# A hybrid decoder block on one core: first half's expert lists paced more slowly, prefix products held behind the sums, first column group read in pairs, selection matrices moved to VectorE

## The chip, the cores and the metric

The kernel runs on one core of a Trainium2 chip. The metric is device time in microseconds (us). TensorE does the matrix products (PE in the rows, PEld its weight loads), VectorE (DVE), ScalarE (ACT) and GpSimd (POOL) the elementwise work, and SyncE (SP) issues most loads. GpSimd also issues the gathers from the expert table.

## The reference

One decoder layer in float32 on 1024 tokens of width 1024. The query width of the expert part is 8 heads x 256.

```
mod = silu(c) @ w_ada + b_ada                      # 6 x 1024: shift, scale, gate, twice
h = modulate(rms_norm(x), shift1, scale1);  proj = h @ w_in
# GLA branch, gMLP branch, sigmoid gates of proj -> merged
x = x + gate1 * (merged @ w_out)
h2 = modulate(rms_norm(x), shift2, scale2)
q = h2 @ w_q                                       # 8 heads, two halves of 128
s1, s2 = q[..., 0, :] @ keys1.T, q[..., 1, :] @ keys2.T     # 128 keys each
idx, g = 16 best of the pairs (top16(s1) + top16(s2)), softmax
u, v = expert_down[idx], expert_up[idx]            # 16384 experts of width 1024
x = x + gate2 * sum(g * gelu(u . h2) * v);  return rms_norm(x)
```

## The kernel before

**Halves.** The tokens are worked in two halves of 512, each four blocks of 128. A half first runs the projection `w_in` in 14 column groups of 512, then the output projection (two parts, `w_out_part`), the second norm (`h2_part`), and the query projection `w_q(q)` in four column groups (`q=0` in two halves of 256 tokens, the others on 512). A column group has eight k-steps (`stream`, `group`): a 128x512 weight tile `wt` is loaded, ScalarE rounds it to `wh` (L1037), GpSimd or VectorE makes the rest `wl` (L1039), and TensorE does twelve products in `mm3` (L173 to L175), so that the float32 product is made of three faster ones. After each k-step `step()` lets four queues go on, each by a credit that the table `rate` gives per step.

**Experts.** Behind a half's query projection `s_part` makes the scores (L1395) and `tops` their best; `rank(b)` puts `routing(b)` of a block into the routing queue, and, at the last block of a group of blocks, `rare(gi)`. The groups are (0,1,2,3), (4,5) and (6,7). Each head's best expert of a token is a direct entry: it is gathered row by row, its dot product is one DVE instruction (L452), and its sum uses the diagonal matrix `Wd`. All other pairs are packed into lists of up to 128 pairs, ten per block; a prefix sum over the 128 partitions gives each pair its place, and the part of it across partitions is the product with `ltri` (L263 in `routing`'s packing and in that of the rare lists, L336 in `rare`). What many tokens of a group share goes through `rare` and its own lists; their result comes back as `yr`, one row in each block's stream.

A list entry takes a selection matrix `E` (L593: a distance `ea` made by ScalarE is compared with a bound), products of `h2` and of the list with `E` (L494, L495, L464, L465), the dot products on VectorE (L496), the gather (L442), a second matrix `e` (L485, named `e2` in the code) that puts its rows back to their tokens, and the sum.

**Two ways of summing.** `peer_stream` goes through one list of entries, `todo`, strictly in its order: the six rare lists of the first group, the lists of blocks 0 to 3 (each closed by its `yr` entry), then for each later group the direct entries, four rare lists, and the lists of its two blocks. The first half's entries run inside the second half's projection, by the credits `RP` (in the projection), `RP2` (output projection and on) and `RP3` (last three query groups). They use small buffers, two entries ahead, and `split_add` (L523 to L526), which splits the gathered values into two parts for faster products. Behind the projection `peer_pools("1", …, True)` opens larger buffers ("own"): seven entries ahead and `add_rows` (L515), float32 products. In own `E`, `e` and `Wr` were made on GpSimd; in the small pool `E` is made on VectorE.

**Start.** `ada_cols(k)` makes the shift and scale of the first norm for 128 columns: it loads 128-column pieces of `w_ada` in runs of 512 bytes, multiplies and adds them on VectorE (L913), and sums over partitions by TensorE. It is called once for each k of the first column group, which cannot pass k before.

The scheduler sets the order on each engine ahead of time; `tc.issue_after(ins)` keeps an instruction behind `ins` on its engine.

Of the kernel before, what the change touches and what calls it, by code (L numbers as in the profile page):

```python
# [54 lines left out]
RP = .42  # L55
RP2 = .42
DA = 8
FP = 15
EP = (True,)
# [9 lines left out]
RP3 = .5  # L69
AS = 1  # L70
# [15 lines left out]
def block_kernel(ctx: ExitStack, tc: tile.TileContext, x, xT, cT, w_ada, b_ada, b_adaT, n1T, w_inp, w_alr,  # L86
# [80 lines left out]

    def split_psum(hi, lo, ps):
        nc.scalar.activation(hi, ps, AF.Identity)  # L169
        nc.vector.tensor_tensor(lo, ps, hi.bitcast(F32), op=OP.subtract)  # L170

    def mm3(ps, lh, ll, rh, rl, first, last):
        nc.tensor.matmul(ps, lh, rh, start=first, stop=False)  # L173
        nc.tensor.matmul(ps, lh, rl, start=False, stop=False)  # L174
        return nc.tensor.matmul(ps, ll, rh, start=False, stop=last).ins  # L175
# [78 lines left out]
    def pack_list(tsel, n, col, rps, tag):  # L254
# [8 lines left out]
        nc.tensor.matmul(pst, ltri, cnt[:, col:col + 1], start=True, stop=True)  # L263
# [62 lines left out]
    def rare(gi, rps):  # L326
# [7 lines left out]
        nc.vector.tensor_copy(cnt[:, col:col + 1], inc[:, n - 1:n])  # L334
        pst = rps.tile([P, 1], F32, name="aux", tag="aux")
        nc.tensor.matmul(pst, ltri, cnt[:, col:col + 1], start=True, stop=True)  # L336
# [122 lines left out]
    def entry_list(pl, ul, Ej, blk):  # L459
# [25 lines left out]
        nc.gpsimd.tensor_scalar(e2, iota[:, int(lane0(b)):int(lane0(b)) + P], ts_[:, 3 * n:3 * n + 1], None, op0=OP.is_equal)  # L485
# [25 lines left out]
    def add_rows(wv, acc, first, last):  # L511
        W, v = wv
        for n in range(2):
            sl = slice(n * 512, (n + 1) * 512)
            nc.tensor.matmul(acc[:, sl], W, v[:, sl], start=first, stop=last)  # L515

    def split_add(ent, acc, first, last):
        pl, _, _, r, uv, _, e2 = ent
        for n in range(2):
# [6 lines left out]
            nc.tensor.matmul(acc[:, sl], e2, vl, start=False, stop=last)  # L526

    def rare_rows(pl, ul, b):
# [4 lines left out]
        nc.gpsimd.tensor_scalar(W, iota[:, :P], rcol[gi][:, bi:bi + 1], None, op0=OP.is_equal)  # L533
# [52 lines left out]
    def peer_E(pl, pb, j):  # L586
# [6 lines left out]
        (nc.gpsimd if pl["own"] in EP else nc.vector).tensor_scalar(E[:, :n], ea[:, :n], hw[:, 1:2], None, op0=OP.is_le)  # L593
# [52 lines left out]
    def peer_stream(bs):  # L646
# [190 lines left out]
    with ExitStack() as pa:  # L837
# [58 lines left out]
        def ada_cols(k):  # L896
            accs = []
            for hf_ in range(2):
                wa = t4("wada").rearrange("p (a c f) -> p a c f", a=4, c=2)
                src = w_ada[hf_ * 512:(hf_ + 1) * 512, :].rearrange("(a p) n -> p a n", p=P)  # L900
                for c in range(2):
                    nc.sync.dma_start(wa[:, :, c], src[:, :, c * D + k * P:c * D + (k + 1) * P])
                acc = gl.tile([P, 2, P], F32, name="adc", bufs=4)
                for a in range(4):
                    w_, s_ = wa[:, a], sc[:, 4 * hf_ + a:4 * hf_ + a + 1]
                    if a < AS:
                        nc.scalar.activation(acc if a == 0 else w_, w_, AF.Identity, scale=s_)
                        if a:
                            nc.gpsimd.tensor_tensor(acc, acc, w_, op=OP.add)
                    elif a == 0:  # L910
                        nc.vector.tensor_scalar(acc, w_, s_, None, op0=OP.mult)
                    else:
                        nc.vector.scalar_tensor_tensor(acc, w_, s_, acc, op0=OP.mult, op1=OP.add)  # L913
                accs.append(acc)
            ps = auxt([P, 2])
            for c in range(2):
                for i, acc in enumerate(accs):
                    nc.tensor.matmul(ps[:, c:c + 1], acc[:, c], ones[:, 0:1], start=i == 0, stop=i == 1)
            nc.vector.tensor_tensor(mod[:, k:16:KD], ps, badat[:, k:16:KD], op=OP.add)
            nc.vector.scalar_tensor_tensor(scol[:, k:k + 1], mod[:, KD + k:KD + k + 1], 1.0, n1t[:, k:k + 1],  # L920
# [80 lines left out]
        def h_first(k):  # L1001
            if k + 1 < KD:
# [491 lines left out]
```

## Time and profile before

| | |
|---|---|
| runs of the kernel (us) | 1672.44, 1666.29, 1671.41; median 1671.41 |
| the profiled execution (us) | 1661.6, of which the span is 1659.9 |
| mean granted clock of TensorE | 0.936 of full speed |
| busy | PE 1438.1 (87%), DVE 1070.9, POOL 887.5, ACT 778.0 |

The profiled execution is 9.8 us under the median of the runs. The span runs from the first to the last instruction; the granted clock is a share of TensorE's full speed.

### The profile page before, as it was taken

How to read it: one execution, taken by the hardware profiler on the slowest of the kernel's cores; microseconds unless marked ns; L12 is line 12 of the kernel's file. 1: busy time of each engine (PE TensorE's matmuls, PEld its weight loads, DVE VectorE, ACT ScalarE, POOL GpSimd, SP SyncE). 2: the span in 40 equal slices, each digit the busy share in tenths (PEclk: the TensorE clock that was granted, in tenths of full speed). 3: DMA queues.
4: the chain of work that ended last, by engine and by line, in shares of the span. 5: the costliest groups of instructions: out<-in, count | busy, mean ns of one | idle time of the engine just before them, and what ended most of it. 6: DMA issues, size and time to landing. Idle time of an engine off the chain costs nothing. (4 is left out here: it accounts for less than half of the span.)

```text
span 1659.9 us, 20529 instructions
## 1 busy us (share of the span) xinstructions
PE 1438.1 (87%) x6113; PEld 1078.2 (65%) x6113; DVE 1070.9 (65%) x2862; ACT 778.0 (47%) x1716; POOL 887.5 (53%) x761
## 2 busy tenths in 40 slices
PE   4999889999998998788889999989789954798894
PEld 2768757888768886567667777767578832353452
DVE  6773654111456469977987778788885476576653
ACT  4453323332446355735446665555455344444442
POOL 4232237543375338756666877556575425655750
PEclk7999989999999999999999999989899975899998
DMA  9643533223377338746756788768756364897992
GB/s 272 235 175 98 173 121 106 93 91 133 101 241 256 119 115 295 251 153 230 260 188 204 282 319 295 281 213 300 275 213 230 114 232 155 346 415 274 410 412 89
DMA packets 132635, 363.83 MB, mean 219 GB/s; under 512 B 17577, under 2 KB 36265, under 8 KB 116386
## 3 DMA queue, kind: packets, MB, share of 16 engines
q0 software_dynamic: 30816, 178.14, 28.5%
q1 hardware_dynamic: 78464, 132.15, 24.2%
q10 hardware_dynamic: 23234, 52.14, 8.8%
q8 instruction: 49, 0.80, 0.2%
q14 instruction: 72, 0.59, 0.1%
HBM read 336.44 MB, written 25.94 MB: 218 GB/s over the span
## 5 line engine op out<-in xcount | busy, mean ns | idle before, releaser
L1039 POOL TENSOR_TENSOR wl<-wt,wh 128x512 fp32r<-128x512 f32 x257 | 364.3, 1424 | 386.5 <-ACT wh L1037 328.1
L174 PE MATMUL mm<-wl,hTh 128*128 128x512 f32 x896 | 366.3, 409 | 10.3 <-DVE wl L1039 5.6
L1037 ACT ACTIVATE wh<-wt 128x512 fp32r<-128x512 f32 x368 | 228.4, 627 | 308.1 <-PE mm L175 184.8
L175 PE MATMUL mm<-wh,hTl 128*128 128x512 f32 x896 | 357.4, 404 | 3.0 <-DVE hTl L996 3.0
L173 PE MATMUL mm<-wh,hTh 128*128 128x512 f32 x896 | 339.5, 413 | 20.2 <-DVE sg L1240 6.4
L173 PEld LDWEIGHTS mm<-wh,hTh 128*128 128x128 f32 x896 | 172.8, 194 | 71.8 <-DVE sg L1240 7.7
L174 PEld LDWEIGHTS mm<-wl,hTh 128*128 128x128 f32 x896 | 173.2, 193 | 59.2 <-POOL wl L1039 9.2
L1039 DVE TENSOR_TENSOR wl<-wt,wh 128x512 fp32r<-128x512 f32 x111 | 100.0, 903 | 158.6 <-ACT wh L1037 146.4
L175 PEld LDWEIGHTS mm<-wh,hTl 128*128 128x128 f32 x896 | 172.6, 193 | 43.3 <-DVE hTl L996 3.1
L173 PE MATMUL mm<-hTh,wh 128*128 128x512 f32 (+1 forms) x448 | 167.2, 375 | 18.7 <-ACT hTh L169 6.4
L175 PE MATMUL mm<-hTh,wl 128*128 128x512 f32 (+1 forms) x448 | 158.2, 371 | 9.7 <-POOL wl L1039 7.2
L174 PE MATMUL mm<-hTl,wh 128*128 128x512 f32 (+1 forms) x448 | 163.9, 366 | 0.0
L442 POOL DMA_INDIRECT uv<-in_tab_dram,ix x94 | 102.7, 1093 | 71.6 <-PE acc L515 24.4
L496 DVE SCALAR_TENSOR_TENSOR uv<-uv,hps 128x512 f32<-128x512 f32 x148 | 97.8, 683 | 54.6 <-PE hps L495 33.3
L524 DVE SCALAR_TENSOR_TENSOR vl<-uv,r,vh 128x512 fp32r<-128x512 f32 x92 | 91.8, 1026 | 34.7 <-ACT vh L523 29.5
L173 PEld LDWEIGHTS mm<-hTh,wh 128*128 128x128 f32 x448 | 86.4, 194 | 35.4 <-ACT hTh L169 7.1
L515 PE MATMUL acc<-uv,W 128*128 128x512 f32 x192 | 98.9, 641 | 4.4 <-ACT W L508 2.9
L175 PEld LDWEIGHTS mm<-hTh,wl 128*128 128x128 f32 x448 | 85.6, 193 | 24.3 <-POOL wl L1039 8.2
L174 PEld LDWEIGHTS mm<-hTl,wh 128*128 128x128 f32 x448 | 86.5, 193 | 13.5 <-DVE hTl L170 0.2
L494 PE MATMUL hps<-hh,E 128*128 128x512 f32 x148 | 77.8, 529 | 17.7 <-DVE uv L496 12.3
L515 PE MATMUL acc<-uv,Wd 128*128 128x512 f32 x128 | 61.3, 628 | 9.1 <-ACT Wd L456 7.2
L186 DVE MAX8 tv<-so 128x8 f32<-128x128 f32 x128 | 28.5, 277 | 62.1 <-ACT so L1397 62.1
(955 smaller groups left out, 2727.9 us busy)
## 6 DMA issues: line engine op xcount, KB each, us to landing
wt<-in_w_inp_dram SPq DMA_DIRECT2D x224, 256.0 KB
wt<-in_w_qp_dram SPq DMA_DIRECT2D x80, 256.0 KB
wada<-in_w_ada_dram SPq DMA_DIRECT2D x32, 512.0 KB
wt<-in_w_outp_dram SPq DMA_DIRECT2D x64, 256.0 KB
wada<-in_w_ada_dram SPq DMA_DIRECT2D x32, 256.0 KB
s_d<-so ACTq DMA_DIRECT2D x32, 256.0 KB
xr<-in_x_dram ACTq DMA_DIRECT2D x8, 512.0 KB
x_d<-x ACTq DMA_DIRECT2D x8, 512.0 KB
```

What stands on the lines that cost most here:

```text
L173: nc.tensor.matmul(ps, lh, rh, start=first, stop=False)
L174: nc.tensor.matmul(ps, lh, rl, start=False, stop=False)
L175: return nc.tensor.matmul(ps, ll, rh, start=False, stop=last).ins
L186: nc.vector.max(v, st)
L442: nc.gpsimd.indirect_dma_start(out=uv[:], out_offset=None, in_=tab, in_offset=bass.IndirectOffsetOnAxis(ap=ix, axis=0))
L494: nc.tensor.matmul(hps, Ej, hh[:, sl], start=True, stop=False)
L496: nc.vector.scalar_tensor_tensor(uv[:, sl], uv[:, sl], 1.0, hps, op0=OP.mult, op1=OP.mult, accum_out=r[:, 2 + n:3 + n])
L515: nc.tensor.matmul(acc[:, sl], W, v[:, sl], start=first, stop=last)
L524: nc.vector.scalar_tensor_tensor(vl, v, r[:, 5:6], vh.bitcast(F32), op0=OP.mult, op1=OP.subtract)
L1037: nc.scalar.activation(wh, wt, AF.Identity)
L1039: eng.tensor_tensor(wl, wt, wh.bitcast(F32), op=OP.subtract)
```

## The change

Six pieces are changed.

1. The credits of the first half's lists go from .42, .42 and .5 to .33, .33 and .3 per step.
2. In own, `E`, `e` and `Wr` are made on VectorE.
3. The products with `ltri` are issued behind the last product that the program wrote before them (a matmul of `mm3`, or a sum), and `rare` yields once ahead of its own.
4. Entries are prepared as far ahead as the buffers of their own block allow, so the first half's last entries stay two ahead behind the projection's end too.
5. `ada_cols` makes 256 columns at a time: 1 KB runs, 128x512 instructions, four calls in place of eight.
6. In the second half, the last query group runs in two halves of 256 tokens, and each half's blocks are ranked at once.

```diff
-RP = .42
-RP2 = .42
+RP = .33
+RP2 = .33
-RP3 = .5
-AS = 1
+RP3 = .3
...
+        last_pe[:] = [nc.tensor.matmul(ps, ll, rh, start=False, stop=last).ins]
+        return last_pe[0]
...
         pst = rps.tile([P, 1], F32, name="aux", tag="aux")
-        nc.tensor.matmul(pst, ltri, cnt[:, col:col + 1], start=True, stop=True)
+        with tc.issue_after(last_pe[0]):
+            nc.tensor.matmul(pst, ltri, cnt[:, col:col + 1], start=True, stop=True)
...
-        nc.gpsimd.tensor_scalar(e2, iota[:, int(lane0(b)):int(lane0(b)) + P], ts_[:, 3 * n:3 * n + 1], None, op0=OP.is_equal)
+        (nc.vector if own else nc.gpsimd).tensor_scalar(e2, iota[:, int(lane0(b)):int(lane0(b)) + P], ts_[:, 3 * n:3 * n + 1], None, op0=OP.is_equal)
...
-        (nc.gpsimd if pl["own"] in EP else nc.vector).tensor_scalar(E[:, :n], ea[:, :n], hw[:, 1:2], None, op0=OP.is_le)
+        nc.vector.tensor_scalar(E[:, :n], ea[:, :n], hw[:, 1:2], None, op0=OP.is_le)
...
         def fill(nxt, k):
-            while nxt < len(todo) and nxt <= k + use[-1]["ahead"]:
+            while nxt < len(todo):
                 b, j = todo[nxt]
+                pl = preps[b][0] if b in preps else use[-1]
+                if nxt > k + pl["ahead"]:
+                    break
...
+        def ada_cols(kp):
             accs = []
+            w2 = 2 * P
             for hf_ in range(2):
+                acc = gl.tile([P, 2, w2], F32, name="adc", bufs=3)
                 for a in range(4):
+                    q = 4 * hf_ + a
+                    if a % 2 == 0:
+                        wa = t4("wada").rearrange("p (a c f) -> p a c f", a=2, c=2)
...
+                    else:
+                        nc.vector.scalar_tensor_tensor(acc, wa[:, a % 2], sc[:, q:q + 1], acc, op0=OP.mult, op1=OP.add)
...
+                for p in (0, 1) if hf and q == 3 else (None,):
+                    w_q(q, p)
+                    if q == 3:
+                        for i in range(BH) if p is None else (2 * p, 2 * p + 1):
+                            rank(blks[i])
...
-            for b in blks:
-                rank(b)
```

TensorE at the end of the second half's projection, before: the last product of the query projection, all scores (`aux<-keyst,qt`), then the first prefix products and direct sums (`Wd`), and at the bottom the first list entry of the later groups.

```order
L175 MATMUL mm<-hTh,wl 128x512
L1395 MATMUL aux<-keyst,qt 128x128 x16
L263 MATMUL aux<-cnt,ltri 128x1
L515 MATMUL acc<-uv,Wd 128x512 x10
L263 MATMUL aux<-cnt,ltri 128x1
L336 MATMUL aux<-cnt,ltri 128x1
L515 MATMUL acc<-uv,Wd 128x512 x4
L349 MATMUL tpq<-tq,qE 128x20
```

The same place in the changed kernel: behind the last product come the scores of two blocks, and then products of the first half's entries (`e_11585` is the matrix of one of them).

```order
L175 MATMUL mm<-hTh,wl 128x256
L1403 MATMUL aux<-keyst,qt 128x128 x8
L529 MATMUL acc<-vh,e_11585 128x512
L530 MATMUL acc<-vl,e_11585 128x512
L529 MATMUL acc<-vh,e_11585 128x512
L468 MATMUL tps<-thl,E 128x170
```

Some sixty rows on, after seven such entries in all, stands the end of the first half's stream (`yr`), and only behind it `rare`'s product (L340, which was L336), the direct sums and the first list of the later groups.

```order
L530 MATMUL acc<-vl,e_12286 128x512
L519 MATMUL acc<-yr,Wr 128x512 x2
L340 MATMUL aux<-cnt,ltri 128x1
L353 MATMUL tpq<-tq,qE 128x20
L519 MATMUL acc<-uv,Wd 128x512 x14
L265 MATMUL aux<-cnt,ltri 128x1
L519 MATMUL acc<-uv,Wd 128x512 x2
L498 MATMUL hps<-hh,E 128x512
```

So seven list entries and one `yr` entry that stood among the projection's products now stand behind the last of them, and the chain of `rare` behind those. The scores of blocks 4 and 5 still stand behind all products of both token halves.

GpSimd in the lists of the last groups, before: gathers (`uv<-in_tab_dram`) alternate with `E` and `e`.

```order
L442 DMA uv<-in_tab_dram,dix_148 128x2048
L166 TENSOR_TENSOR fs<-fs,mhalf 128x1
L593 TENSOR_SCALAR E<-ea,hw 128x256 x3
L442 DMA uv<-in_tab_dram,dix_148 128x2048
L593 TENSOR_SCALAR E<-ea,hw 128x256
L442 DMA uv<-in_tab_dram,dix_148 128x2048
L485 TENSOR_SCALAR e_13719<-iota,ts__13709 128x128
L485 TENSOR_SCALAR e_13741<-iota,ts__13731 128x128
L442 DMA uv<-in_tab_dram,ix 128x2048
```

The same stretch of GpSimd after:

```order
L446 DMA uv<-in_tab_dram,ix 128x2048
L446 DMA uv<-in_tab_dram,dix_148 128x2048 x3
L164 TENSOR_TENSOR fs<-fs,mhalf 128x1
L446 DMA uv<-in_tab_dram,dix_148 128x2048 x5
L277 TENSOR_TENSOR tlq<-qtsel,thq 128x32
L164 TENSOR_TENSOR fs<-fs,mhalf 128x1
L446 DMA uv<-in_tab_dram,ix 128x2048
L446 DMA uv<-in_tab_dram,dix_149 128x2048 x2
```

Gathers and three small instructions are left on GpSimd there. The matrices stand on VectorE now, between the dot products of the lists (L500, which was L496).

```order
L500 SCALAR_TENSOR_TENSOR uv,r<-uv,hps 128x512
L489 TENSOR_SCALAR e_14488<-iota,ts__14478 128x128
L474 SCALAR_TENSOR_TENSOR jk,r<-ts__14538,slot_65 128x56
L500 SCALAR_TENSOR_TENSOR uv,r<-uv,hps 128x512
L486 SCALAR_TENSOR_TENSOR jk,r<-ts__14538,slot_65 128x56
L500 SCALAR_TENSOR_TENSOR uv,r<-uv,hps 128x512
L489 TENSOR_SCALAR e_14509<-iota,ts__14499 128x128
```

Here two `e` of 128x128 stand where VectorE had dot products and `jk` alone.

## Rows read from the trace of the kernel before

**Rows 1.** The page's busy us, share of the span and instructions of each engine.

```profile
PE 1438.1 (87%) x6113; PEld 1078.2 (65%) x6113; DVE 1070.9 (65%) x2862; ACT 778.0 (47%) x1716; POOL 887.5 (53%) x761
```

**Rows 2.** Windows by stage: busy us (instructions) of each engine, clock, DMA share, GB/s.

```profile
30.00:46.00 16.00, 11.06 (x28) 8.29 (x29) 15.97 (x23) 7.42 (x13) 11.09 (x8) 0.50 0.79 224
46.00:75.00 29.00, 29.00 (x148) 22.49 (x146) 19.27 (x39) 16.20 (x27) 6.85 (x10) 0.99 0.64 225
250.00:417.00 167.00, 163.32 (x726) 131.69 (x725) 36.26 (x66) 55.82 (x86) 87.56 (x65) 0.99 0.32 106
417.00:510.00 93.00, 81.78 (x357) 63.66 (x356) 50.58 (x64) 43.08 (x75) 45.54 (x35) 0.95 0.56 190
...
870.00:1060.00 190.00, 179.53 (x801) 143.09 (x800) 145.49 (x306) 115.14 (x276) 136.43 (x116) 0.98 0.80 292
1060.00:1250.00 190.00, 161.54 (x764) 128.13 (x763) 164.52 (x295) 106.30 (x227) 120.70 (x91) 0.93 0.68 239
1250.00:1337.00 87.00, 86.49 (x432) 72.04 (x430) 38.72 (x187) 36.12 (x68) 37.16 (x29) 1.00 0.44 153
1337.00:1392.00 55.00, 19.77 (x42) 8.17 (x42) 45.68 (x294) 27.39 (x68) 18.51 (x30) 0.68 0.51 191
1392.00:1440.00 48.00, 32.67 (x87) 20.08 (x88) 30.21 (x149) 22.37 (x78) 35.45 (x37) 0.69 0.78 297
1440.00:1500.00 60.00, 57.78 (x178) 31.20 (x177) 40.23 (x186) 26.85 (x85) 33.38 (x39) 1.00 1.01 413
1500.00:1560.00 60.00, 47.70 (x129) 23.72 (x127) 37.19 (x125) 27.44 (x95) 40.60 (x43) 0.89 0.83 315
1560.00:1608.00 48.00, 45.03 (x134) 22.83 (x132) 27.77 (x97) 22.13 (x74) 27.88 (x30) 1.00 1.01 421
1608.00:1650.00 42.00, 29.45 (x84) 15.01 (x82) 20.62 (x48) 12.21 (x34) 5.96 (x8) 0.93 0.48 183
```

**Rows 3.** Groups of the first 46 us by line: busy us, mean ns, idle before.

```profile
L913 DVE SCALAR_TENSOR_TENSOR adc<-wada,sc,adc 128x256 f32<-128x256 f32 x29 | 19.8, 731 | 1.7 <-ACT adc L907 1.7
```

**Rows 4.** TensorE's timeline at the projection's end: start, us, line, idle before and releaser.

```profile
1334.90 2.05 PE L1395 MATMUL aux<-keyst,qt 128*128 128x128 f32 x16 [0.46 <-ACT so L1397]
1353.31 0.56 PE L263 MATMUL aux<-cnt,ltri 128*128 128x1 f32 x2 [16.35 <-DVE cnt L260]
1353.73 10.81 PE L515 MATMUL acc<-uv,Wd 128*128 128x512 f32 x20
...
1365.52 0.36 PE L336 MATMUL aux<-cnt,ltri 128*128 128x1 f32 x2
...
1388.51 0.59 PE L263 MATMUL aux<-cnt,ltri 128*128 128x1 f32 x2 [11.46 <-DVE cnt L260]
1391.96 0.80 PE L494 MATMUL hps<-hh,E 128*128 128x512 f32 x1 [2.87 <-POOL E L593]
```

**Rows 5.** Groups of VectorE, 870 to 1250 us.

```profile
L524 DVE SCALAR_TENSOR_TENSOR vl<-uv,r,vh 128x512 fp32r<-128x512 f32 x84 | 84.8, 1036 | 29.7 <-ACT vh L523 24.4 <-PE acc L526 2.9 <-PE acc L525 1.4
...
L593 DVE TENSOR_SCALAR E<-ea,hw 128x128 fp32r<-128x128 f32 x40 | 23.0, 576 | 3.2 <-PE hps L495 2.1 <-ACT ea L592 1.1
```

**Rows 6.** Groups of TensorE, 870 to 1250 us: products of the halved column group.

```profile
L173 PE MATMUL mm<-hTh,wh 128*128 128x256 f32 x64 | 18.8, 297 | 7.4 <-DVE hTl L170 5.3 <-ACT hTh L169 2.2
```

**Rows 7.** Groups behind 1392 us, GpSimd, VectorE and TensorE.

```profile
L593 POOL TENSOR_SCALAR E<-ea,hw 128x256 fp32r<-128x256 f32 x23 | 25.8, 1122 | 4.0 <-ACT ea L592 3.6 <-PE hps L495 0.2
L485 POOL TENSOR_SCALAR e<-iota,ts__12915 128x128 f32<-128x128 f32 x1 | 2.5, 2527 | 0.0
L496 DVE SCALAR_TENSOR_TENSOR uv<-uv,hps 128x512 f32<-128x512 f32 x96 | 63.3, 684 | 34.7 <-PE hps L495 21.2 <-DMA uv<-in_tab_dram,ix 13.1 <-issue 0.2
```

**Rows 8.** Waits, 1392 to 1440 us, then 1500 to 1560 us: total, times, longest.

```profile
ACT ea L592 <- POOL E L593: 7.1, 5, 2.2
...
ACT ea L592 <- POOL E L593: 11.8, 7, 2.3
```

**Rows 9.** One line of VectorE (comparison with a constant, 128x128): min, median, max ns.

```profile
L345 DVE TENSOR_SCALAR qlt<-iota,qse x3: 266/280/288, 768.9 to 1456.9; 128x128 f32<-128x128 f32 x3
```

More of the change, by code (lines that the diff above doesn't have):

```diff
@@ L514, in add_rows @@
             sl = slice(n * 512, (n + 1) * 512)
-            nc.tensor.matmul(acc[:, sl], W, v[:, sl], start=first, stop=last)
+            last_pe[:] = [nc.tensor.matmul(acc[:, sl], W, v[:, sl], start=first, stop=last).ins]
     def split_add(ent, acc, first, last):
@@ L532, in rare_rows @@
         W = pl["pq"].tile([P, P], F32, name="Wr", tag="e2", bufs=pl["ahead"] + 2)
-        nc.gpsimd.tensor_scalar(W, iota[:, :P], rcol[gi][:, bi:bi + 1], None, op0=OP.is_equal)
+        (nc.vector if pl["own"] else nc.gpsimd).tensor_scalar(W, iota[:, :P], rcol[gi][:, bi:bi + 1], None, op0=OP.is_equal)
         return W, y
@@ L894, in ada_acc @@
                 yield acc
-        def ada_cols(k):
+        def ada_cols(kp):
             accs = []
+            w2 = 2 * P
             for hf_ in range(2):
[L899 to L903, printed above, removed]
-                for a in range(4):
[L905 to L911, printed above, removed]
+                acc = gl.tile([P, 2, w2], F32, name="adc", bufs=3)
+                for a in range(4):
+                    q = 4 * hf_ + a
+                    if a % 2 == 0:
+                        wa = t4("wada").rearrange("p (a c f) -> p a c f", a=2, c=2)
+                        src = w_ada[q * P:(q + 2) * P, :].rearrange("(a p) n -> p a n", p=P)
+                        for c in range(2):
+                            nc.sync.dma_start(wa[:, :, c], src[:, :, c * D + kp * w2:c * D + (kp + 1) * w2])
+                    if a == 0:
+                        nc.scalar.activation(acc, wa[:, 0], AF.Identity, scale=sc[:, q:q + 1])
@@ L912, in ada_cols @@
                     else:
-                        nc.vector.scalar_tensor_tensor(acc, w_, s_, acc, op0=OP.mult, op1=OP.add)
+                        nc.vector.scalar_tensor_tensor(acc, wa[:, a % 2], sc[:, q:q + 1], acc, op0=OP.mult, op1=OP.add)
                 accs.append(acc)
-            ps = auxt([P, 2])
+            ps = auxt([P, 2, 2])
             for c in range(2):
-                for i, acc in enumerate(accs):
-                    nc.tensor.matmul(ps[:, c:c + 1], acc[:, c], ones[:, 0:1], start=i == 0, stop=i == 1)
@@ L919, in ada_cols @@
-            nc.vector.tensor_tensor(mod[:, k:16:KD], ps, badat[:, k:16:KD], op=OP.add)
-            nc.vector.scalar_tensor_tensor(scol[:, k:k + 1], mod[:, KD + k:KD + k + 1], 1.0, n1t[:, k:k + 1],
+                for j in range(2):
+                    for i, acc in enumerate(accs):
+                        nc.tensor.matmul(ps[:, c, j:j + 1], acc[:, c, j * P:(j + 1) * P], ones[:, 0:1], start=i == 0, stop=i == 1)
+            ks = slice(2 * kp, 2 * kp + 2)
+            nc.vector.tensor_tensor(mod.rearrange("p (c k) -> p c k", c=2)[:, :, ks], ps,
+                                    badat.rearrange("p (c k) -> p c k", c=2)[:, :, ks], op=OP.add)
```

15 lines of the change are left out of this document (8 added, 7 removed).

## The prediction

> **What bounds the kernel now.** I read the page first, then a table of windows by stage, then the waits and TensorE's timeline where a stage loses time. The page: TensorE is busy for 1438 of 1659.9 us, VectorE for 1071, so TensorE is the one to look at, but neither is full [rows 1]. The windows show four kinds of stage [rows 2].
>
> - The start: at 30 to 46 us VectorE is busy for all 16 us while TensorE does 11.06 us at half clock, 5.5 us of work at full clock. From 46 on TensorE is full.
> - The projections: TensorE bound. The first half's, without lists, is idle for 14.9 of the 260 us from 250 to 510. The second half's, with lists in it, is idle for 38.9 of the 380 us from 870 to 1250, at clocks of .98 and .93. Behind 1250, when the lists are done, it is full again: 86.49 of 87.
> - The zone behind the projection, 1337 to 1392: VectorE is busy for 45.7 of 55 us, with routing, direct dots and packing. TensorE works 19.8 us; the last scores end at 1336.95, the first list entry of the later groups comes at 1391.96 [rows 2, 4].
> - The lists behind it: in two stretches the DMA engines are full (share 1.01, 413 and 421 GB/s); in two others, 1392 to 1440 and 1500 to 1560, they are not, and TensorE idles 15.3 and 12.3 us [rows 2]. There ScalarE's `ea` waits for GpSimd's `E`, 7.1 and 11.8 us [rows 8].
>
> **The change part by part**, against the profiled execution of 1661.6 us.
>
> *Column pairs at the start: −6.* VectorE does 48 `adc` instructions of 256 columns; 29 of them lie in the first 46 us at 731 ns, 19.8 us [rows 3]. The pairs need 24 of 512 columns. A 128x512 instruction of the same kind takes 684 ns [rows 7], so the whole is 16.4 us against 35. At full clock the stretch from 30 to 46 can give back at most 16 − 5.5 = 10.5 us, since TensorE is full behind it [rows 2]. But the first k-step now needs two columns' weights: one extra megabyte, at 224 to 278 GB/s some 4 us, and the first step comes later by that. I take −6, with −10 and +4 as the ends.
>
> *Lists paced more slowly.* Forty-six list entries run in the small buffers; 42 of them lie between 870 and 1250 (84 `vl`, two per entry [rows 5]). The order shows seven of the 46, and one `yr` entry, behind the last projection product after the change. One entry is eight products of 512 columns and some short ones; in the projection a product takes 163.32 / 726 = .225 us [rows 2], so 1.9 us, and seven are 13; with `yr` **−14** of TensorE's work in a full stretch. Then the stalls: with the first half's idle share (14.9 / 260, times 380) 870 to 1250 would lose 21.8 us, and lost 38.9; the clock (.99 and .95 against .98 and .93) costs some 8 us more. That makes 25 us for 42 entries, .6 us each, 28 us for 46. Thirty-nine at .33 / .42 = .79 of the density, with stalls in proportion to the density, give 39 x .6 x .79 = 18.5: **−9**. The ends are 0 (the stall belongs to the entry, and fills 1250 to 1337 in turn) and −20 (it vanishes when entries stand apart).
>
> *Last query group in halves: +3.* Sixteen k-steps in place of eight, with the same columns for TensorE but eight more tiles to load, round and split. ScalarE and GpSimd have the room: 36 and 37 of 87 us [rows 2]. The halved group of before idled 7.4 us ahead of its steps [rows 6]; the ends are 0 and +7. The earlier ranking buys nothing that I count: the scores of blocks 4 and 5 still stand behind every product.
>
> *The zone behind the projection: +22.* Seven entries put 14 `vl` and 14 dots on VectorE there; their sum with routing and the direct dots that stand ahead of `rare` in the order is 51 us by before's durations (for instance 14 dots at .68, seven direct dots at 1.2). `rare`'s product now comes behind the `yr` entry; from it to the first list entry took 1391.96 − 1365.52 = 26.4 us [rows 4], and this chain of DMA and small VectorE work stays. So 77 us in place of 55. Low end +10: the entries fill VectorE's 9 idle us and `rare`'s waits. High end +35: they run as they did inside the projection, 380 / 42 = 9 us each, 63 us, then `rare`'s chain. The gathers cannot use the time, as the direct entries fill the seven that may be ahead.
>
> *Prefix products behind sums: 0 by themselves.* Their waits of 16.35 and 11.46 us hold nothing up: the `Wd` products queued behind the first come with the routing at 1353, and the list behind the second needs that prefix [rows 4]. What the hold does, putting `rare` behind `yr`, is in the zone's term. Without that cover it would cost up to the 26.4 us of `rare`'s chain.
>
> *Matrices on VectorE: −16.* Behind 1392 the windows move 48 x .297 + 60 x .413 + 60 x .315 + 48 x .421 + 42 x .183 = 85.8 MB; at 417 GB/s that is 206 us of 258 [rows 2]. Of the 52 us lost, 23 are in the last window, which is running dry; the other 29 lie in the two stretches in which `ea` waits for `E` on GpSimd. `E` takes 1122 ns there for two entries and `e` up to 2527 [rows 7], queued with gathers. On VectorE `E` takes 576 ns for one [rows 5], and a like comparison 280 [rows 9]. I take a little over half of the 29, since the filling behind 1392 stays. VectorE, at 40.2 of 60 us in the full stretch [rows 2], has room: at .3 us for each of two matrices some 20 entries add 12 us; at .6 they add 24 and the room is gone (a rival below). The ends are −25 and +5.
>
> The rest (preparing two ahead for the old entries) is inside the zone's term. Sum: −6 − 14 − 9 + 3 + 22 − 16 = −20, so 1641.6 where the profile had 1661.6. The median of the runs stands 9.8 us above that execution; I add them: **1651 us**.
>
> **The rivals.**
>
> *The gain is larger: 1628.* TensorE is idle for 35 us in the zone, and if the leftovers hide there the zone costs only +10; stalls fall to the end of −20. Then −6 − 14 − 20 + 3 + 10 − 16 = −43, and 1618.6 + 9.8 is 1628. For it: VectorE idles 9 us there and `rare` waits for DMA. Against: VectorE, not TensorE, is the zone's limit.
>
> *It comes out even: 1672.* Relief on GpSimd is nothing (something else is late as soon as `E` is early), stalls fall by 4 only: −6 − 14 − 4 + 3 + 22 + 0 = +1. For it: it is ScalarE that waits for `E`, and its 7.1 and 11.8 us [rows 8] are not TensorE's. Against it: both stretches with such waits are those with idle DMA engines, and the two without are full [rows 2].
>
> *Slower: 1705, by VectorE in the lists.* An entry gathers 128 x 2048 floats, 1.05 MB, which at 417 GB/s takes 2.5 us. Behind 1392 there are 48 lists (96 dots [rows 7]). VectorE has two dots of .68, their reads and short `jk` for each, some 1.9 us. If `E` and `e` run at .6 each, as `E` did with gathers beside it [rows 5], and the dots are slowed by a like amount on top, the period becomes 3.3 us, and 48 lists cost .8 x 48 = +38 in place of the −16: −6 − 14 − 9 + 3 + 22 + 38 = +34, 1705. The side changes at a small excess: without relief the sum is −4, and .09 us on each list takes that back; .26 us makes it slower by 0.5%. Against it: VectorE's 20 idle us in the full stretch. The rows speak for it only weakly: with `E` on VectorE beside gathers in the projection it took 576 ns for 128 columns, where a like instruction took 280 [rows 5, 9]; what it does to a full queue of gathers no row shows. Beside this stands a rule of the Trainium skill (SBUF — State Buffer, section "Who interferes with whom"): VectorE and GpSimd share a port pair, a `tensor_scalar` on VectorE can take it for its whole length, and the descriptors of a gather on GpSimd then wait. By that rule the time would be this rival's.
>
> **How the numbers follow.** Chances: forecast .43 (1635 to 1665 its own range), larger gain .20, even .25, slower .12. A measurement of this kernel tells about 0.5% (8.4 us) from no change, so faster means under 1663, slower over 1679.8. Faster: nine tenths of the forecast's .43, all of .20 and a quarter of the even case, .65. Slower: the .12 and a little of the even case, .14. Same: .21. The range goes to 1615 below (the larger gain, with −10 at the start) and 1685 above (the even case with the zone's +35); the slower case's 1705 is left out.
>
> **What would show it.** The step to look at is the zone: the first list entry of the later groups some 77 us behind the last scores, with seven `vl` pairs in it. 870 to 1250 should idle near 30 us, and 1250 to its end should have lists. Behind the zone, `ea` should wait for nothing on GpSimd and the DMA share be near 1 all through but at the end. At the start `adc` should be some 16 us in all. Wrong would be a zone that is no longer than before, lists of more than 2.8 us each behind the zone, or a second stage that falls back to a lower clock.

## The result and the profile after

The changed kernel took 1684.28 us (median of four runs, 1676.65 to 1686.85) where the kernel before took 1668.85: the ratio is 1.0089, with a 95% interval of 1.006 to 1.0118. It is slower; 1651 had been forecast, and 1685 was the range's upper end. The profiled execution took 1683.67 us and its span is 1681.6, so the two traces are 22 us apart where the medians are 15 apart: some 7 us of the differences between the two traces below are not the change's.

The page's busy time, as in [rows 1]:

```profile
PE 1464.5 (87%) x6209; PEld 1091.5 (65%) x6209; DVE 1064.6 (63%) x2910; ACT 791.6 (47%) x1721; POOL 818.1 (49%) x689
```

The windows of the changed kernel, in the columns of [rows 2]. Since every stage has moved, the later ones are cut at its own events: last projection product 1312.5, end of the first half's stream 1382.7, first list of the later groups 1407.2.

```profile
30.00:46.00 16.00, 13.53 (x44) 10.01 (x45) 15.83 (x14) 6.61 (x11) 13.63 (x9) 0.61 0.79 267
...
870.00:1060.00 190.00, 176.94 (x780) 140.13 (x779) 129.85 (x280) 109.64 (x256) 125.46 (x105) 0.98 0.74 266
1060.00:1250.00 190.00, 172.73 (x833) 138.10 (x832) 140.20 (x266) 107.22 (x215) 109.33 (x86) 0.94 0.66 228
...
1250.00:1312.50 62.50, 59.56 (x370) 52.46 (x369) 40.92 (x160) 29.52 (x65) 40.74 (x32) 0.97 0.58 200
1312.50:1382.70 70.20, 39.42 (x105) 22.66 (x104) 53.40 (x272) 33.18 (x81) 21.28 (x28) 0.59 0.58 223
1382.70:1407.20 24.50, 17.34 (x38) 7.55 (x36) 19.83 (x98) 10.20 (x26) 8.69 (x13) 0.77 0.39 137
...
1500.00:1528.00 28.00, 22.95 (x65) 11.50 (x63) 22.18 (x99) 13.73 (x35) 10.60 (x11) 1.00 1.00 408
1528.00:1552.00 24.00, 16.30 (x39) 7.52 (x40) 15.88 (x43) 12.43 (x36) 0.82 (x2) 0.93 0.43 169
1552.00:1608.00 56.00, 47.32 (x127) 24.33 (x125) 32.95 (x136) 23.38 (x85) 22.08 (x22) 0.85 0.93 376
```

Two stretches stand out. From 1312.5 to 1407.2 TensorE works 57 of 95 us, at a clock of .59 and .77, and VectorE is not full either. From 1528 to 1552 the DMA engines, at a share of 1.00 ahead of it and .93 behind it, fall to .43, and GpSimd is busy for .82 us.

Both traces have the same events, so the loss can be put down stage by stage. Times are read from TensorE's timeline, in us, to .1 or .2: the end of the first half's scores, the start of the last projection product, the start of the first list of the later groups, the end of the last sum.

| | before | changed | length before | length changed | difference |
|---|---|---|---|---|---|
| first half's scores end | 623.4 | 618.1 | 623.4 | 618.1 | −5.3 |
| last projection product | 1332.2 | 1312.5 | 708.8 | 694.4 | −14.4 |
| first list of the later groups (zone) | 1392.0 | 1407.2 | 59.8 | 94.7 | +34.9 |
| last sum (lists) | 1639.6 | 1662.0 | 247.7 | 254.7 | +7.0 |
| end | 1659.9 | 1681.6 | 20.3 | 19.6 | −0.7 |

The first two stages gained 19.7 us and the zone and the lists lost 41.9. TensorE in the zone, as in [rows 4]:

```profile
1340.05 3.76 PE L1403 MATMUL aux<-keyst,qt 128*128 128x128 f32 x16
...
1378.56 0.79 PE L530 MATMUL acc<-vl,e 128*128 128x512 f32 x1 [2.88 <-DVE vl L528]
1379.22 3.75 PE L519 MATMUL acc<-yr,Wr 128*128 128x512 f32 x4
1382.77 0.43 PE L340 MATMUL aux<-cnt,ltri 128*128 128x1 f32 x2
...
1407.21 0.50 PE L498 MATMUL hps<-hh,E 128*128 128x512 f32 x1 [0.32 <-DVE E L597]
```

The seven list entries that are left over from the first half (the leftovers) and `yr` take until 1382.8, 70 us behind the last product, and `rare`'s chain another 24.4. The chain of work shows how the first part ends:

```profile
1359.24 11.57 DMA uv<-in_tab_dram,ix
...
1374.32 3.52 DVE uv L456 x6
1377.84 0.68 DVE vl L528
1378.52 0.26 issue
1378.78 6.05 DMA uv<-in_tab_dram,dix
1384.85 1.34 DVE uv L456 x2
```

The last leftover's gather takes 11.57 us from issue to landing, among the gathers of the direct entries (`dix`); its `vl` then stands behind direct dots (L456) on VectorE; and the last direct entry's gather, issued behind that `vl`, lands at 1384.8.

### The profile page after: what moved, and what is told of

It is laid out like the page before. It is cut to its first block, busy times and chain, and to the rows that moved or that the text cites. A ratio compares the mean times of both kernels' runs of the same rounds, so it can differ in the third digit from the quotient of the medians.

```text
span 1681.6 us, 20678 instructions
## 1 busy us (share of the span) xinstructions
PE 1464.5 (87%) x6209; PEld 1091.5 (65%) x6209; DVE 1064.6 (63%) x2910; ACT 791.6 (47%) x1721; POOL 818.1 (49%) x689
## 4 chain that ended last, share of the span: by engine, by line
PE 45%; DVE 22%; DMA 13%; issue 8%; ACT 6%; POOL 3%; ACTq 0%; another core or an unknown queue 0%; SPq 0%; DVEq 0%; POOLq 0%
PE mm L174 10%; PE mm L173 10%; PE mm L175 10%; PE acc L519 6%; DMA uv<-in_tab_dram,ix 4%; DMA wada<-in_w_ada_dram 3%; PE hps L498 2%; DVE uv L500 1%; POOL wl L1047 1%; DVE wl L1047 1%; PE hps L499 1%; PE aux L1403 1%; DVE vl L528 1%; DMA fin<-y_d 1%; DVE yd L644 1%
## 5 line engine op out<-in xcount | busy, mean ns | idle before, releaser
L1047 POOL TENSOR_TENSOR wl<-wt,wh 128x512 fp32r<-128x512 f32 x264 | 372.7, 1419 | 386.8 <-ACT wh L1045 367.3
L1047 DVE TENSOR_TENSOR wl<-wt,wh 128x512 fp32r<-128x512 f32 x112 | 94.6, 846 | 181.2 <-ACT wh L1045 174.8
L173 PE MATMUL mm<-hTh,wh 128*128 128x512 f32 (+1 forms) x480 | 175.5, 368 | 12.8 <-ACT hTh L169 4.6
L174 PE MATMUL mm<-hTl,wh 128*128 128x512 f32 (+1 forms) x480 | 171.7, 359 | 0.2 <-DVE hTl L170 0.2
L175 PE MATMUL mm<-hTh,wl 128*128 128x512 f32 (+1 forms) x480 | 164.3, 360 | 8.5 <-POOL wl L1047 7.8
L500 DVE SCALAR_TENSOR_TENSOR uv<-uv,hps 128x512 f32<-128x512 f32 x148 | 98.0, 683 | 66.9 <-PE hps L499 36.5
L173 PEld LDWEIGHTS mm<-hTh,wh 128*128 128x128 f32 x480 | 94.5, 197 | 28.8 <-ACT vt L1092 5.5
L528 DVE SCALAR_TENSOR_TENSOR vl<-uv,r,vh 128x512 fp32r<-128x512 f32 x92 | 86.0, 966 | 38.0 <-ACT vh L527 37.1
L175 PEld LDWEIGHTS mm<-hTh,wl 128*128 128x128 f32 x480 | 92.7, 196 | 22.6 <-POOL wl L1047 9.3
L174 PEld LDWEIGHTS mm<-hTl,wh 128*128 128x128 f32 x480 | 94.7, 197 | 13.3 <-DVE hTl L170 0.9
L498 PE MATMUL hps<-hh,E 128*128 128x512 f32 x148 | 79.8, 541 | 25.4 <-DVE uv L500 18.9
L502 ACT ACTIVATE r<-r 128x1 f32<-128x1 f32 x74 | 21.7, 294 | 103.4 <-DVE uv L500 93.5
```

The source lines that it names most:

```text
L175: last_pe[:] = [nc.tensor.matmul(ps, ll, rh, start=False, stop=last).ins]
L498: nc.tensor.matmul(hps, Ej, hh[:, sl], start=True, stop=False)
L500: nc.vector.scalar_tensor_tensor(uv[:, sl], uv[:, sl], 1.0, hps, op0=OP.mult, op1=OP.mult, accum_out=r[:, 2 + n:3 + n])
L502: nc.scalar.activation(r[:, 4:5], r[:, 2:3], AF.Gelu, bias=r[:, 3:4])
L528: nc.vector.scalar_tensor_tensor(vl, v, r[:, 5:6], vh.bitcast(F32), op0=OP.mult, op1=OP.subtract)
L1047: eng.tensor_tensor(wl, wt, wh.bitcast(F32), op=OP.subtract)
```

## The experiments

All kernels compute the whole result. "Lists" is the time from the first list of the later groups to the last sum, "zone" that from the last projection product to that list, read from each kernel's own trace; the ratios are against the kernel before. "Hold" is the third piece of the change, which keeps a product with `ltri` behind another product. All are gathered here first.

| run | what differs | ratio (95% interval) | last product | zone | lists |
|---|---|---|---|---|---|
| changed kernel | | 1.0089 (1.0060 to 1.0118) | 1312.5 | 94.7 | 254.7 |
| e1 | changed, matrices on GpSimd | 1.0181 (1.0157 to 1.0204) | 1314.1 | 94.9 | 267.5 |
| e2 | changed, no hold | 0.9998 (0.9981 to 1.0014) | 1312.9 | 96.2 | 238.3 |
| e3 | changed, old credits | 0.9919 (0.9896 to 0.9941) | 1324.1 | 56.0 | 250.9 |
| e4 | before, column pairs | 0.9987 (0.9969 to 1.0004) | 1330.8 | 58.1 | 252.9 |
| e5 | changed, old credits, no hold | 0.9951 (0.9929 to 0.9973) | 1338.7 | 54.4 | 247.0 |
| e6 | before, matrices on VectorE | 0.9968 (0.9948 to 0.9989) | 1337.4 | 59.2 | 245.0 |
| e7 | before, last query group halved | 1.0041 (1.0021 to 1.0061) | 1339.2 | 54.5 | 258.5 |
| e8 | changed, no hold, old depth | 1.0015 (1.0000 to 1.0030) | 1311.2 | 88.1 | 248.7 |
| e9 | e3, last query group whole | 0.9965 (0.9943 to 0.9986) | 1327.4 | 60.2 | 258.4 |
| e10 | before, hold | 1.0113 (1.0078 to 1.0147) | 1337.3 | 61.3 | 267.3 |
| e11 | before, credits and depth | 1.0135 (1.0110 to 1.0160) | 1314.7 | 100.9 | 248.8 |
| e12 | changed, no hold on rare's own | 1.0079 (1.0057 to 1.0101) | 1308.3 | 96.5 | 252.7 |
| e13 | before, hold but on the last group | 1.0020 (1.0001 to 1.0038) | 1337.0 | 61.4 | 251.9 |
| e14 | before, hold on the last group alone | 1.0114 (1.0088 to 1.0141) | 1339.8 | 59.1 | 269.2 |
| e15 | changed, no hold on the last group | 0.9984 (0.9962 to 1.0006) | 1315.2 | 95.0 | 237.9 |
| e16 | e3, no hold on the last group | 0.9878 (0.9851 to 0.9905) | 1327.7 | 56.0 | 242.5 |

**e1, matrices back on GpSimd.**

```diff
-(nc.vector if own else nc.gpsimd).tensor_scalar(e2, ...)
+nc.gpsimd.tensor_scalar(e2, ...)
-nc.vector.tensor_scalar(E[:, :n], ea[:, :n], hw[:, 1:2], None, op0=OP.is_le)
+(nc.gpsimd if pl["own"] else nc.vector).tensor_scalar(E[:, :n], ea[:, :n], hw[:, 1:2], None, op0=OP.is_le)
```

> The changed kernel with E, e and Wr of the last groups back on GpSimd; all else changed. Against the kernel before the whole change stands at 1.009 (+15 us). From the first list of the later groups to the last sum the change took 254.7 us, before 247.7. Theory A (VectorE carries the matrices badly, so this is where the predicted gain went): that stretch falls back to 248 us or below, ratio about 1.004. Theory B (the zone behind the projection is the whole loss; which engine makes the matrices does not matter): the stretch stays within 3 us of 255, ratio 1.007 to 1.011.

Both theories fell: the kernel became slower by another 0.9%, 12.8 us of it in the lists. The matrices on VectorE were not where the gain went; their size here is the one forecast. VectorE behind 1407 in the changed kernel, its group of `E` and its longest `e`:

```profile
L597 DVE TENSOR_SCALAR E<-ea,hw 128x256 fp32r<-128x256 f32 x24 | 8.6, 357 | 10.9 <-ACT ea L596 7.9 <-PE hps L499 3.0
...
L489 DVE TENSOR_SCALAR e<-iota,ts__12888 128x128 f32<-128x128 f32 x1 | 0.4, 440 | 0.0
```

`E` takes 357 ns where GpSimd took 1122 [rows 7], and 440 ns is the longest of the 48 `e`.

**e2, no hold.**

```diff
-        with tc.issue_after(last_pe[0]):
-            nc.tensor.matmul(pst, ltri, cnt[:, col:col + 1], start=True, stop=True)
+        nc.tensor.matmul(pst, ltri, cnt[:, col:col + 1], start=True, stop=True)
```

> The changed kernel without the ordering edge on the products with ltri (and without the extra yield in rare). In the order rare's product for the later group then stands one entry and the yr entry earlier. Theory C (the hold puts rare's chain, 24.4 us from its product to the first list, behind the first half's stream): the first list of the later groups comes some 10 to 15 us earlier than 94.7 us behind the last projection product, ratio about 1.001. Theory D (the leftovers themselves, at 9.4 us each, set the zone): 0 to 5 us earlier, ratio 1.006 to 1.009.

The ratio is that of theory C, but its place is wrong: the zone is as long as before (96.2 us), and the lists are 16.4 us shorter. In this kernel the hold costs some 15 us, behind the zone.

**e3, the old credits.**

```diff
-RP = .33
-RP2 = .33
+RP = .42
+RP2 = .42
-RP3 = .3
+RP3 = .5
```

> The changed kernel with the old credits .42, .42 and .5. No list entry of the first half then stands behind the last projection product. Theory D: the zone from the last projection product to the first list of the later groups shrinks from 94.7 us to some 60 as before, the last product comes 8 to 14 us later; net 20 us less, ratio about 0.996. Rival (what the slower pace gives in the projection outweighs what it costs behind it): ratio above 1.009.

Theory D holds, and by more than it expected: the zone is 38.7 us shorter, the last product comes 11.6 us later, and the ratio falls by 0.017. This version beats both kernels.

**e4, the pairs alone** (the new `ada_cols` in the kernel before).

> The kernel before with the pairs of columns at the start alone. If the start gives what the milestones of the changed kernel show (the first half's last scores 5.3 us earlier), ratio 0.996 to 0.998. Rival: the order of everything behind shifts and the gain is lost, ratio 0.999 or more.

1.0 is just inside the interval. The first half's scores end 6.8 us earlier in its trace, and the lists are 5.2 us longer for no reason in the change; differences of 5 us in one stage of one trace are therefore not read as effects below. The start itself does not rest on one trace: in the eleven traces with the pairs the first half's scores end between 616.5 and 620.5 us, in the seven without between 621.6 and 624.7.

**e5, e6, e7, e8: two undone, two alone, and the depth.** e5 is e2 and e3 together. e6 is the VectorE lines of e1's diff, put into the kernel before. e7 puts the two halves of the last query group and the ranking behind each into the kernel before. e8 is e2 with

```diff
-            while nxt < len(todo):
+            while nxt < len(todo) and nxt <= k + use[-1]["ahead"]:
                 b, j = todo[nxt]
-                pl = preps[b][0] if b in preps else use[-1]
-                if nxt > k + pl["ahead"]:
-                    break
```

> The changed kernel with the old credits and without the hold: what is left of the change are VectorE's matrices, the column pairs and the halved last query group. The credits cost 1.0089 - 0.9919 = 0.017, the hold 1.0089 - 0.9998 = 0.009 of the time before. If the two act in different places (the credits in the zone, the hold in the lists behind), both come off: ratio 0.981 to 0.985, some 1638 us, with the lists of the later groups at some 235 us in place of 251. Rival (the hold costs only where the leftovers have made the groups late): ratio 0.990 to 0.993, lists at 250 us.

> The kernel before with E, e and Wr of the last groups on VectorE and nothing else. With the matrices put back to GpSimd the changed kernel became 0.009 slower, 12.8 us of it in the lists. If that is the matrices' worth in either order: ratio 0.988 to 0.992, lists 232 to 238 us in place of 247.7. Rival (they help only where VectorE has been made idle by late groups): ratio 0.996 or more.

> The kernel before with the last query group in two halves and the ranking behind each, and nothing else. In its order two prefix products, six direct sums and the scores of two blocks stand ahead of the other scores, and the first two blocks' scores ahead of the last products. Prediction's view (costs 3 us and buys nothing): ratio 1.001 to 1.003. Rival (two blocks' routing starts beside the last products, so the zone is shorter than 59.8 us by 5 or more): ratio 0.996 to 0.999.

> The changed kernel without the hold, and with the preparing depth of before: behind the projection seven entries ahead for all, so also for the seven leftovers of the first half. It stood at 0.9998 with two ahead, and its leftovers came 9.4 us apart in a zone of 96 us. Theory E (two ahead paces the leftovers): they come 5 us apart or less, the zone is 20 us or more shorter, ratio 0.985 to 0.990. Rival (VectorE and ScalarE pace them, or three small buffers do): ratio 0.998 to 1.002.

e5 missed: the two do not add up. Without the hold the lists fall by 4 us, where 16 had been expected, and the last product comes 14.6 us later than with it. e6: the matrices alone are worth 0.3%, a third of what they are worth in the changed kernel. e7: the halves alone cost 0.4%, more than either view had it; the zone is 5 us shorter, the last product 7 us later, and the lists are 10.8 us longer, for which no run gives a reason. e8: seven entries ahead instead of two make the zone 8 us shorter in the trace and the kernel no faster, as the rival had it; the leftovers still come 8.6 us apart (9.6 in e2), so the depth is at most a small part of what paces them.

**e9, e10, e11, e12.** e9 is e3 with `w_q(3)` whole and the ranking behind it. e10 is the hold of e2's diff, put into the kernel before; e11 the new credits with the depth of the changed `fill`, put into the kernel before; e12 takes the hold from the product in `rare` only.

> The changed kernel with the old credits and the last query group whole again; the hold, VectorE's matrices and the column pairs stay. With the halves it stood at 0.9919, and the halves alone cost the kernel before 0.0041. If that cost is the same here: ratio 0.986 to 0.989. Rival (with the matrices on VectorE the earlier scores of two blocks are worth their 8 us): ratio 0.992 to 0.996.

> The kernel before with the hold on the ltri products alone. With the old credits, and everything else of the change, the hold was worth 0.003 (0.9919 with it, 0.9951 without): the projection 14.6 us shorter, the lists 3.9 longer. Theory F (without leftovers of the first half the hold is harmless or helps): ratio 0.994 to 1.000. Rival (it delays rare's chain in the lists whatever stands ahead): ratio 1.004 or more.

> The kernel before with the new credits and the preparing depth that goes with them, nothing else. Its order has the seven leftovers and yr behind the last projection product, the prefix products behind them but the scores among them. Theory D (the credits trade some 23 us of projection for some 35 us of zone): the last product 20 to 25 us earlier, the first list of the later groups 8 to 15 us later than 1392, ratio 1.004 to 1.010. Rival (without hold and halves the zone hides them): ratio 0.990 to 0.998.

> The changed kernel with the hold kept on the blocks' own prefix products and taken from rare's alone (its yield kept). Theory C2 (the hold's 15 us are rare's chain of the last group: its product came at 1485 us in place of 1448, 37 us later, and the gathers behind it): ratio 0.999 to 1.002, lists at 240 us. Rival (the blocks' prefix products are what is late): ratio 1.006 to 1.009, lists at 254 us.

Three of the four ended on the rival's side, e9 by a hair past its range; e11 went beyond what theory D gave. e9: the halves, which cost 0.4% alone, are worth 0.5% in this company. e10: the hold alone costs 1.1%, nearly all of it in the lists, 267.3 us in place of 247.7. e11: the credits alone cost 1.35%, a zone of 100.9 us in place of 59.8 against a last product that comes 17.5 us earlier. e12: the late product is not that of `rare` itself.

**e13 to e16, which of the held products.** The hold is put on, or taken from, the four products of the last group (blocks 6 and 7, their rare lists, and `rare`'s own for that group). The diff is the edit of e15 and e16 in the packing; in `rare` the condition is `gi < 2`. e13 puts the hold into the kernel before with the same two conditions, e14 with the opposite ones. The extra `yield` in `rare` is in all four.

```diff
-        with tc.issue_after(last_pe[0]):
+        with tc.issue_after(last_pe[0]) if col not in (6, 7, NBLK + 2) else ExitStack():
             nc.tensor.matmul(pst, ltri, cnt[:, col:col + 1], start=True, stop=True)
```

> The kernel before with the hold on all ltri products but the four of the last group (blocks 6 and 7, their rare lists, and rare's own). The hold alone made it 1.0113, all of it in the lists (267.3 us in place of 247.7), and its last group's products came 29 to 34 us later. Theory G (the last group's products, held behind the sums of the groups before it, are the cost): ratio 0.998 to 1.003, lists at 246 to 253 us. Rival (the hold costs through the first of the late groups or by shifting everything): ratio 1.007 or more.

> The complement: the kernel before with the hold on the four products of the last group alone. Theory G: ratio 1.009 to 1.013, lists at 263 to 269 us, GpSimd waiting for thq of the last rare lists. Rival: ratio 1.003 or less.

> The changed kernel with the hold taken from the four products of the last group alone. Without any hold it stood at 0.9998, without rare's at 1.0079, as it is at 1.0089. Theory G: ratio 0.999 to 1.003, lists at 238 to 243 us in place of 254.7. Rival: 1.006 or more.

> The version with the old credits that stood at 0.9919, with the hold taken from the last group's four products. Theory G, if the projection keeps its shorter time (last product at 1324 us) and the lists lose 4 us of 250.9: ratio 0.988 to 0.990. Rival (the shorter projection belongs to one particular order and goes when anything is changed, as it did without the hold, last product at 1338.7): ratio 0.994 to 0.997.

Theory G held in all four; three numbers lie just past the ranges given (e14's lists 269.2 us, e15's ratio and lists .9984 and 237.9, e16's ratio .9878). The place is seen in TensorE's timelines. In the kernel before, the last group's product runs among list entries, 17 us ahead of the `yr` entry of the group before and of the last group's first direct sums:

```profile
1498.79 0.28 PE L263 MATMUL aux<-cnt,ltri 128*128 128x1 f32 x2
...
1515.66 2.94 PE L515 MATMUL acc<-yr,Wr 128*128 128x512 f32 x4
1519.65 3.70 PE L515 MATMUL acc<-uv,Wd 128*128 128x512 f32 x8 [1.05 <-ACT Wd L456]
```

In e14 it runs behind both:

```profile
1522.88 3.20 PE L521 MATMUL acc<-yr,Wr 128*128 128x512 f32 x4
1525.92 1.88 PE L521 MATMUL acc<-uv,Wd 128*128 128x512 f32 x4
1527.64 0.28 PE L267 MATMUL aux<-cnt,ltri 128*128 128x1 f32 x2
...
1547.17 8.21 PE L521 MATMUL acc<-uv,Wd 128*128 128x512 f32 x12 [11.23 <-ACT Wd L462]
```

In e13, with the last group free, it runs among the list entries of the group before again:

```profile
1509.16 0.39 PE L501 MATMUL hps<-hl,E 128*128 128x512 f32 x1
1509.39 0.28 PE L267 MATMUL aux<-cnt,ltri 128*128 128x1 f32 x2
```

That is 18 us earlier than in e14; GpSimd's `tlq`, which needs what the product leads to, waits .32 us there, and in e14 6.23.

The changed kernel shows the same pattern. TensorE, ScalarE and GpSimd from their timelines:

```profile
1524.33 1.88 PE L519 MATMUL acc<-yr,Wr 128*128 128x512 f32 x4
1528.70 1.98 PE L519 MATMUL acc<-uv,Wd 128*128 128x512 f32 x4 [2.49 <-ACT Wd L460]
1530.52 0.28 PE L265 MATMUL aux<-cnt,ltri 128*128 128x1 f32 x2
...
1544.25 7.08 PE L519 MATMUL acc<-uv,Wd 128*128 128x512 f32 x12 [5.09 <-ACT Wd L460]
```

```profile
1535.15 0.25 ACT L276 ACTIVATE thq<-qtsel 128x50 fp32r<-128x50 f32 x1
...
1535.59 0.49 ACT L596 ACTIVATE ea<-iota,mid 128x256 f32<-128x256 f32 x1
...
1542.09 0.51 ACT L596 ACTIVATE ea<-iota,mid 128x256 f32<-128x256 f32 x1 [0.42 <-DVE E L597]
...
1543.80 0.40 ACT L460 ACTIVATE Wd<-ident,rd 128x128 f32<-128x128 f32 x1
```

```profile
1526.01 0.94 POOL L446 DMA_INDIRECT uv<-in_tab_dram,dix  x1 [0.31 <-issue]
1535.48 0.25 POOL L277 TENSOR_TENSOR tlq<-qtsel,thq 128x32 fp32r<-128x32 f32 x1 [8.53 <-ACT thq L276]
1548.08 0.56 POOL L164 TENSOR_TENSOR fs<-fs,mhalf 128x1 f32<-128x1 f32 x1 [12.35 <-DVE fs L163]
```

The product is held until the `yr` entry and the first direct sum of the group have run. From it come the packed list (`thq`, `tlq`) and the `mid` of the last lists, and with these eight `ea` one after another on ScalarE, each but the first waiting .42 us for VectorE's `E`. The next `Wd` stands behind all eight, at 1543.8, and TensorE's sums wait for it. GpSimd, whose order is set ahead too, waits 8.53 us for `thq` and issues no gather between 1527 and 1552. The same window in e15, with those four products free, has a DMA share of .76 in place of .43 and 22.68 us of TensorE's work in place of 16.30:

```profile
1528.00:1552.00 24.00, 22.68 (x62) 10.74 (x60) 16.98 (x51) 10.34 (x41) 11.14 (x10) 0.95 0.76 266
```

## Why the prediction was wrong, step by step

**Column pairs (−6).** About right: the first half's scores end 5.3 us earlier, and 30 to 46 us holds 13.53 us of TensorE's work in place of 11.06. The reason was only half right. The 24 instructions of 512 columns took 23.6 us in all, not 16.4: they ran at 1000 ns on average, not at the 684 of an instruction that the prediction took for a like one (its second input lies in PSUM). Eighteen of them ran at 749 ns; the six that ran while GpSimd worked on tiles took 1754 (rows at the end). The kernel as a whole gained 0.1% by the pairs alone (e4), which cannot be told from nothing.

**Credits: −14 and −9 in the projection.** Right as far as one trace of each kernel can tell. From the first half's scores to the last product the changed kernel took 14.4 us less (694.4 for 708.8), where −14 − 9 + 3 = −20 had been forecast. The trace of the kernel before is on the short side there: e6, e10, e13 and e14, in which TensorE goes through the same products in the same order for nearly all of that stage, took 713.9, 713.8, 715.4 and 716.5 us. e11, the credits alone, took 690.0 (1314.7 − 624.7): 18.8 us less than the trace before, 24 to 26 less than those four. The stalls fell as forecast too: TensorE idles 30.3 us between 870 and 1250, where 30 had been said and 38.9 was before.

**The zone (+22, high end +35).** This is one of the two steps that failed: +34.9 in the changed kernel, 38.7 by e3, 41.1 by e11. The sum took 51 us of VectorE's work and set it equal to the time. VectorE did work 53.4 us there, as counted, but over 70.2. The chain shown above for the last leftover is one of gather, dot, `vh`, `vl` and sum, in which pieces stand in line behind routing or direct entries; that this is what paces all seven is argued from that trace and not shown by a run of its own. `rare`'s chain behind it was 24.4 us as said (26.4). The size came out at the bound that the prediction had set aside as an extreme, 9 us per entry: `yr` was done 70 us behind the last product. That this bound fits may be chance. Inside the projection the credits set the pace of the entries (42 of them between 870 and 1250 before, 36 after), and behind it no credit does. The sign that had been named, 77 us from the last scores to the first list, came out at 63.4, but the scores of the last two blocks now stand behind three leftovers, 27.5 us behind the last product (1340.05), so the zone as a whole is what tells. Taking the credits back removes the zone's growth and 1.7% of the time, so this trade, some 20 us of projection against 35 to 41 of zone, is the larger loss.

**The hold (0).** This is the other step that failed, and the one that was wrong in kind: some 15 us by e2, 19 alone by e10. The prediction looked at the waits on prefix products in the zone, where it found that a late product delays nothing, and priced the hold there. It did not look at the same line in the lists, where the last group's product ran among list entries (1498.79, without idle time before it) and now stands behind `yr` and a direct sum. e13 and e14 put the cost on those four products (1.0020 without them, 1.0114 with them alone), e15 does so in the changed kernel. With the old credits and the rest of the change, what the hold costs as a whole does not show (e3 at 0.9919 with it, e5 at 0.9951 without, in intervals that overlap), although its last group seems to cost 0.4% there too (e3 against e16).

**Halves (+3).** Alone they cost 7 us by the ratio of e7. In the projection they may well cost the forecast 3: e7's 717.4 us there (1339.2 − 621.8) are 1 to 4 more than in the four traces above. e9 against e3 has them gain 0.5%, with the old credits as in e7, so it is the rest of the company (hold, matrices, pairs, depth) that changes the sign, and which part of it was not tried. Whether the earlier ranking buys anything in the changed kernel itself no run tells.

**Matrices on VectorE (−16).** The size was right in the changed kernel (15 us by e1); in the kernel before it is a third of that (e6, 5 us). The reason was wrong in the main, so the size is in part luck. In e6 no `ea` waits for a matrix on GpSimd any more, and the two stretches that had been put down to these waits, each 4.5 us later there, look much as they did [rows 2]:

```profile
1396.50:1444.50 48.00, 32.22 (x84) 18.95 (x85) 32.93 (x170) 23.00 (x79) 14.35 (x16) 0.70 0.74 286
...
1504.50:1564.50 60.00, 48.98 (x139) 24.23 (x138) 44.02 (x161) 29.00 (x100) 20.73 (x22) 0.94 0.91 347
```

TensorE idles 15.8 and 11.0 us in them, before 15.3 and 12.3. In the changed kernel some of the gain is relief from the hold: the eight `ea` behind the held product wait for `E`, and with `E` on GpSimd (e1) TensorE's sums behind them wait 10.79 us for `Wd`, where the changed kernel waits 5.09:

```profile
1558.45 5.72 PE L519 MATMUL acc<-uv,Wd 128*128 128x512 f32 x8 [10.79 <-ACT Wd L460]
```

The forecast that the DMA engines would be near full all through did not come true either (.43 from 1528 to 1552).

**The rivals.** The slower one forecast lists paced by VectorE; the trace refutes it (`E` 357 ns, `e` mostly under 300). The rule of the Trainium skill (SBUF — State Buffer, section "Who interferes with whom") that stood beside it did not show in the gathers: with all matrices on VectorE their instructions on GpSimd took 978 ns behind 1407, 1054 in the kernel before and 990 in e1, and the DMA engines reached a share of 1.00 (1500 to 1528). The kernel was slower by two mechanisms, of which one was in the sum with too small a price and one was priced at nothing. That 1684 lies just inside the range, which ended at 1685, is luck: that end was made of no gain from the matrices and a zone of +35, with nothing for the hold; the matrices gave 15 us, and the hold took about as much.

**Still open.** Why e5's projection ends 14.6 us later than e3's and 11 later than e16's, with the same credits: the hold on the other products goes with a shorter projection there, but in the kernel before (e10, e13) it does not. Which instructions change places for it was not followed up. What paces the leftovers was not taken apart beyond the depth (e8). Where the halves' cost in e7 and their gain in e3 come from is open too.

## What to carry to other kernels

An engine's load in a stretch bounds its length from below only: where entries pass one by one through four engines that also do other work, 53 us of VectorE's work took 70 us here. An ordering edge has to be priced at every place where its line runs, above all where the line so far waits for nobody: the four products that cost 19 us take some .3 us each. A wait that a view shows is not yet a cost: taking away the 18.9 us for which `ea` waited on GpSimd gave the kernel before 5 us (e6). Parts of a change have to be tried apart and in company: here the credits alone and the hold alone each cost as much as the whole or more, the halves changed sign with the company, and the best version (e16: matrices on VectorE, pairs, halves, the hold off the last group, old credits) runs at 0.988 of the time before.

## What was not expected of the hardware

A comparison with a constant on 128x256 took 357 ns on VectorE where GpSimd took 1122, and the gathers on GpSimd beside it took 978 ns where the same 48 took 1054 before (990 in e1, which has the matrices on GpSimd): VectorE's comparisons did not slow the gathers measurably there.

At the start, on the other hand, VectorE was slowed. The 24 `adc` instructions of the changed kernel (128x512, two inputs) took 1000 ns on average, and this average hides two levels. The eighteen ahead of 25 us and behind 43 took 749 ns. The six between 28.9 and 42.5 us took 1754; GpSimd worked on 128x512 tiles without a pause from 26.0 to 43.6 us, and hardly at all while the others ran.

The group of the gathers behind 1407 us, and those of `adc` from 0 to 25, from 26 to 43 and from 43.3 to 75 us, all of the changed kernel:

```profile
L446 POOL DMA_INDIRECT uv<-in_tab_dram,ix x48 | 46.9, 978 | 108.2 <-PE acc L519 30.7 <-PE hps L499 21.6 <-ACT ix L477 19.0
...
L918 DVE SCALAR_TENSOR_TENSOR adc<-wada,sc,adc 128x512 f32<-128x512 f32 x9 | 6.6, 749 | 0.3 <-ACT adc L916 0.2
...
L918 DVE SCALAR_TENSOR_TENSOR adc<-wada,sc,adc 128x512 f32<-128x512 f32 x6 | 10.3, 1754 | 0.0
...
L918 DVE SCALAR_TENSOR_TENSOR adc<-wada,sc,adc 128x512 f32<-128x512 f32 x9 | 6.7, 749 | 0.2
```

The DMA engines were no busier while the six ran (a share of .79 from 30 to 46 us, .95 from 0 to 30), so their load does not explain it. That GpSimd's work is the reason is read from the times; no run takes that work away.
